# Differential-attention scores of layer 0 as three products of rounded and low parts, with the low parts kept in the residual tiles and tile 1's scores computed beside tile 3's

## The chip, the cores and the metric

One core of one Trainium2 chip runs the whole program. The metric is the device time of one execution in microseconds (us); the time before is the median of 3 runs, 1106.02 us (1105.82 to 1106.52). One further execution was taken by the profiler, and every duration below is from it.

## What is computed

The reference is a decoder trunk of two layers on 512 tokens of width 1024 in float32. Layer 0 runs latent attention (8 heads) and differential attention (4 heads) side by side behind one input projection, joins their outputs in one output projection, adds the result to the residual stream `x`, and is followed by a gated ConvFFN. Layer 1 has other attentions and the same ConvFFN. The change lies in the differential attention of layer 0:

```python
def block(args):
    i, a1, a2 = args                 # one tile of 128 queries, two query halves
    dist = (qpos[:, None] - kpos[None, :]).astype(jnp.float32)
    bias = -slopes[:, None, None] * dist
    def probs(qb, kf):
        s = jnp.einsum('bhqd,bhkd->bhqk', qb, kf).astype(jnp.float32) * scale + bias
        return jax.nn.softmax(jnp.where(causal, s, -jnp.inf), axis=-1)
    p = probs(a1, k1) - lam * probs(a2, k2)
    return jnp.einsum('bhqk,bhkd->bhqd', p.astype(v.dtype), v)
...
x = x + rms_norm(h, ev_post_g[j])    # after the output projection
```

## The kernel before

The tokens are four tiles of 128 (`i` = 0 to 3, `NT` = 4). `X[i]` is a tile's row of the residual stream (128 x 1024 float32), kept in SBUF from its first load (`load_x`, L141) until layer 0's attention output is added to it.

**Products.** TensorE multiplies plain float32 operands directly (an f32 matmul), or float32r operands, which are float32 numbers rounded to fewer bits. `mm3` (L318 to L322) makes an accurate product of rounded operands: high x high, then the two products with one high and one low part, where low = value - high. Weights come as raw tiles over SP's DMA queue (`wraw<-`, L61, three raw buffers of 512 KB), are cast to `wh` on ScalarE (L83, ACT) and give `wl` by a subtract on VectorE (L84, DVE). Activations that are used so are cut by `split` (L225 on ACT, L226 on DVE).

**The stage.** `even()` (L860) is layer 0's attention. Its differential heads run from about 112 to 200 us in 16 units `n` = (head `h`, query tile `i`), four heads with `i` in the order 3, 2, 0, 1, and four more iterations that drain. PE, DVE, ACT and POOL execute it in the order in which the loop at L1389 writes it; the DMA issues on SP stand outside that order, and a scheduler places them. One iteration `n` issues:

1. `score(n)` (L1256): for both halves `z` an f32 matmul of 64 contraction rows (row group `z`) into one PSUM bank each, `sps<-dqk` (L1265); 128 queries by (i+1)*128 keys. The unit `i` = 2 computes tile 0's scores as well, in columns 384 to 512 of its banks, and the unit `i` = 0 only picks them up. DVE adds the distance term and finds the minimum (L1275).
2. perhaps a weight cast and subtract (L83, L84).
3. `exps(n)` on ACT (L1282).
4. `fill(before)`: steps of work that does not depend on the heads at hand. A step is one `mm3` of 512 columns, or three matmuls. First come the query and key projections of heads 1 to 3 (`qk_parts`, `aqk`, eight steps each, closed by one DVE operation L1360 that writes `dqk`), then the output projection (`parts_of`, `ao`), whose weights `ev_w_out` arrive meanwhile.
5. `turn(n-1)`: transposes `tpp<-ident,s` (L891) of the combined weights; `value(n-2)`: `o<-dv,pt` (L1300), its scaling and squares on ACT, `rr` on POOL (L1307), and one long POOL DMA (L163) that prepares the ConvFFN's weights in DRAM.
6. `fill(behind)`; `norm(n-4)` on DVE (`otok`, L1314); `combine(n)` on DVE (L1287 to L1289), which gives `s` to the transposes of the next iteration; every fourth time `finish` of a head (L1321).

`plan` holds the pair (before, behind) of each iteration: (6, 2), then eleven times (2, 2), four times (2, 1), and the drain. The projections of head 0 (`diff_qk`, L1029) stand in an earlier part of `even()`, near 40 to 50 us. After the loop the output projection ends tile by tile (3, 2, 1, 0), its result is normed and added to `X[i]` (L1441), and `X[i]` is spilled to DRAM (L617).

Of the kernel before, what the change touches and what calls it, by code (L numbers as in the profile page):

```python
# [9 lines left out]
F32 = mybir.dt.float32  # L10
# [87 lines left out]
def trunk(tc, A, out):  # L98
# [3 lines left out]
    with ExitStack() as top:  # L102
# [757 lines left out]
        def even():  # L860
            with ExitStack() as es:
                ap = es.enter_context(tc.tile_pool(name="ea", bufs=1, reuse_waits="tile"))
                dqk = [ap.tile([P, 2, S], F32, tag=f"dqk{h}", name=f"dqk{h}") for h in range(4)]
                dq, dk = [t[:, 0] for t in dqk], [t[:, 1] for t in dqk]
                dv = ap.tile([P, NT, 512], F32, tag="dv", name="dv")
                oM = (ap.tile([P, 4, S], F32R, tag="omh", name="omh"),
                      ap.tile([P, 4, S], F32R, tag="oml", name="oml"))

                zero = dqk[0][:, 0, :P]
# [30 lines left out]
                with ExitStack() as e1:  # L900
# [137 lines left out]
                    with e2:  # L1038
                        qtab = cp.tile([P, 2, S], F32, tag="qtab", name="qtab")
# [216 lines left out]
                def score(h, i):  # L1256
                    if i == ORDER[0]:
                        otoks[h] = sc.tile([P, NT, P], F32, tag="otok", name="otok2", bufs=2)
                    w = (i + 1) * P
                    if i:  # L1260
                        ps = [bank("s", "sps") for _ in range(2)]
                        for j, c in ((2, slice(0, 384)), (0, slice(384, 512))) if i == 2 else ((i, slice(0, w)), ):
                            for z in range(2):
                                r = slice(z * 64, (z + 1) * 64)
                                PE.matmul(ps[z][:, c], dq[h][r, j * P:(j + 1) * P], dk[h][r, :c.stop - c.start],  # L1265
                                          start=True, stop=True)
                        if i == 2:
                            ahead[h] = [p[:, 384:] for p in ps]
                        ps = [p[:, :w] for p in ps]
                    else:  # L1270
                        ps = ahead.pop(h)
# [79 lines left out]
                def qk_parts(h, z):  # L1351
                    acc = bank("a", "aqk")
                    wh, wl = W.next()
                    for k in range(KD):
                        mm3(acc, wh[:, k * P:(k + 1) * P], wl[:, k * P:(k + 1) * P], xh[:, k], xl[:, k],
                            k == 0, k == KD - 1)
                        if k < KD - 1:
                            yield
                    scale = 1.0 if z else -0.125 / SLOPES[h]
                    DVE.scalar_tensor_tensor((dk if z else dq)[h], acc, scale, r_row, ALU.mult, ALU.mult)  # L1360
                    yield


# [17 lines left out]

                units = [(h, i) for h in range(4) for i in (3, 2, 0, 1)]
                moves = sum_steps(0, range(3, 5))
                scored, turned_, valued = {}, {}, {}
# [612 lines left out]
```

## Time and profile before

| | us |
|---|---|
| median of 3 runs | 1106.02 |
| profiled execution, its time | 1108.29 |
| its span, first to last instruction | 1106.5 |
| mean granted TensorE clock | 0.998 |
| TensorE busy | 1097.4 (99%) |
| VectorE busy | 896.6 (81%) |
| ScalarE busy | 641.4 (58%) |
| DMA, mean rate | 197 GB/s |

The profiled execution is 2.27 us above the median; 1.8 us of it lie outside the span. A row of the timeline gives the start in us, the length in us, the engine, the kernel's line, the operation, output<-inputs, the shapes and the count of instructions; in brackets the idle time before it and what ended it. Consecutive matmuls overlap in these rows, so that what one costs is read from start to start. PEld is the weight load of TensorE, which runs beside the matmul before it. SPq is SP's sequencer, with the moment at which a transfer is issued.

### The profile page before, as it was taken

The page shows a single profiled execution, that of the slowest core. Times are in us where ns is not written, and L with a number is a line of the kernel's source. Part 1 is how long each engine was busy: PE and PEld are TensorE (multiplying, and loading weights), DVE is VectorE, ACT ScalarE, POOL GpSimd, SP SyncE. Part 2 cuts the span into 40 slices and gives each one's busy share as a digit, 9 for nine tenths or more (in the row PEclk, how much of TensorE's full clock was granted, in tenths as well). Part 3 has the DMA queues.
Part 4 walks back from the last instruction along what each step waited for, and adds up shares of the span by engine and source line. Part 5 has one row for each costly group of instructions (what it writes and reads, how often), then busy time and mean ns, then how long its engine had stood idle before and what let it go on. Part 6 is the DMA issues. An engine that isn't in the chain of part 4 may idle for free.

```text
span 1106.5 us, 17950 instructions
## 1 busy us (share of the span) xinstructions
PE 1097.4 (99%) x6688; PEld 955.6 (86%) x6688; DVE 896.6 (81%) x1509; ACT 641.4 (58%) x1094; POOL 129.2 (12%) x246
## 2 busy tenths in 40 slices
PE   9999999999999999999999999999999999999997
PEld 8876777898999999888878877788999999988886
DVE  6666676489899999999874765458989999999897
ACT  6555566346666666556544555556566666656562
POOL 3311143320000000000032111014100000000002
PEclk9999999999999999999999999999999999999999
DMA  7897898458456555354627999858656555535462
GB/s 273 255 239 210 228 282 236 109 188 219 159 182 191 175 188 181 124 179 136 236 96 259 288 289 299 228 167 246 197 161 191 177 181 186 184 123 161 152 208 78
DMA packets 72600, 217.51 MB, mean 197 GB/s; under 512 B 10048, under 2 KB 11200, under 8 KB 64320
## 3 DMA queue, kind: packets, MB, share of 16 engines
q1 hardware_dynamic: 61872, 147.99, 40.3%
q0 software_dynamic: 9920, 67.12, 24.1%
q10 hardware_dynamic: 720, 1.25, 0.4%
q8 instruction: 53, 0.87, 0.3%
q14 instruction: 35, 0.29, 0.1%
HBM read 208.95 MB, written 73.43 MB: 255 GB/s over the span
## 4 chain that ended last, share of the span: by engine, by line
PE 89%; DVE 6%; DMA 2%; ACT 1%; issue 1%; POOL 0%; POOLq 0%; DVEq 0%; ACTq 0%; SPq 0%
PE u L322 12%; PE u L320 12%; PE u L321 12%; PE acc L321 4%; PE acc L320 4%; PE acc L322 4%; PE apt L320 3%; PE apt L321 3%; PE apt L322 3%; PE ao L320 2%; PE ao L322 2%; PE ao L321 2%; PE aqk L320 1%; DVE wl L84 1%; PE p L321 1%; PE p L320 1%
## 5 line engine op out<-in xcount | busy, mean ns | idle before, releaser
L84 DVE TENSOR_TENSOR wl<-wraw,wh 128x1024 fp32r<-128x1024 f32 x246 | 298.0, 1218 | 34.3 <-ACT wh L83 33.8
L83 ACT CAST wh<-wraw 128x1024 fp32r<-128x1024 f32 x246 | 254.2, 1046 | 102.4 <-PE u L321 21.5
L322 PE MATMUL u<-xh,wl 128*128 128x256 f32 (+1 forms) x640 | 194.9, 305 | 0.0
L321 PE MATMUL u<-xl,wh 128*128 128x256 f32 (+1 forms) x640 | 194.7, 304 | 0.0
L320 PE MATMUL u<-xh,wh 128*128 128x256 f32 (+1 forms) x640 | 194.5, 305 | 0.0
L322 PEld LDWEIGHTS u<-xh,wl 128*128 128x128 f32 x640 | 122.3, 191 | 5.5 <-DVE wl L84 0.7
L321 PEld LDWEIGHTS u<-xl,wh 128*128 128x128 f32 x640 | 122.3, 191 | 4.9
L320 PEld LDWEIGHTS u<-xh,wh 128*128 128x128 f32 x640 | 122.2, 191 | 5.0
L320 PE MATMUL u<-gh,wh 128*128 128x256 f32 x384 | 108.7, 283 | 0.0
L322 PE MATMUL u<-gh,wl 128*128 128x256 f32 x384 | 108.7, 283 | 0.0
L321 PE MATMUL u<-gl,wh 128*128 128x256 f32 x384 | 108.7, 283 | 0.0
L321 PE MATMUL acc<-wl,gh 128*128 128x512 f32 (+1 forms) x234 | 90.9, 389 | 0.1
L322 PE MATMUL acc<-wh,gl 128*128 128x512 f32 (+1 forms) x234 | 90.7, 387 | 0.0
L320 PE MATMUL acc<-wh,gh 128*128 128x512 f32 (+1 forms) x234 | 90.3, 388 | 0.0
L233 POOL TENSOR_TENSOR rv<-ms,epst 128x1 f32<-128x1 f32 x31 | 12.4, 399 | 617.8 <-ACT junk L287 286.2
L484 ACT ACTIVATE y<-u,cw 128x512 f32<-128x512 f32 x88 | 67.6, 776 | 27.5 <-PE u L322 27.5
L321 PEld LDWEIGHTS u<-gl,wh 128*128 128x128 f32 x384 | 73.7, 192 | 0.1
L320 PEld LDWEIGHTS u<-gh,wh 128*128 128x128 f32 x384 | 73.7, 192 | 0.1
L322 PEld LDWEIGHTS u<-gh,wl 128*128 128x128 f32 x384 | 73.7, 192 | 0.0
L163 POOL DMA_DIRECT2D ws<-in_ffn_up_q x72 | 51.7, 720 | 158.7 <-DMA ws<-ws 81.9
L490 DVE SCALAR_TENSOR_TENSOR y<-u,cw,y 128x510 f32<-128x510 f32 x88 | 65.5, 746 | 2.2
L488 DVE SCALAR_TENSOR_TENSOR y<-u,cw,y 128x511 f32<-128x511 f32 x88 | 64.9, 742 | 0.8 <-ACT y L484 0.8
(382 smaller groups left out, 2458.6 us busy)
## 6 DMA issues: line engine op xcount, KB each, us to landing
ws<-in_ffn_up_q POOLq DMA_DIRECT2D x48, 768.0 KB, 12.8
wraw<-ws SPq DMA_DIRECT2D x128, 256.0 KB, 2.9
wraw<-in_ffn_up_q SPq DMA_DIRECT2D x96, 256.0 KB, 2.9
wraw<-in_ffn_w_down SPq DMA_DIRECT2D x44, 512.0 KB, 3.6
ws<-ws POOLq DMA_DIRECT2D x16, 768.0 KB, 13.1
ws<-in_ffn_up_q POOLq DMA_DIRECT2D x24, 512.0 KB, 7.4
wraw<-in_ffn_w_up SPq DMA_DIRECT2D x24, 512.0 KB, 4.4
wraw<-in_od_w_dqk SPq DMA_DIRECT2D x12, 512.0 KB, 9.2
```

The lines of the kernel that those rows point to most:

```text
L83: self.nc.scalar.copy(h[:, :w], raw[:, :w])
L84: self.nc.vector.tensor_tensor(l[:, :w], raw[:, :w], h[:, :w].bitcast(F32), ALU.subtract)
L163: nc.gpsimd.dma_start(tiles[j][c][:].rearrange(wide, q=4), src.rearrange(wide, q=4), accum_op=op, max_dma_last_dim=8192)
L233: POOL.tensor_tensor(v[:, :n], ms, eps[:, :n], ALU.add)
L320: PE.matmul(o, lh, rh, start=first, stop=False, skip_group_check=more)
L321: PE.matmul(o, lh, rl, start=False, stop=False, skip_group_check=more)
L322: PE.matmul(o, ll, rh, start=False, stop=last, skip_group_check=more)
L484: ACT.activation(y[:, z], u[z], AF.Identity, bias=c[:, 3:4], scale=c[:, 2:3])
L488: DVE.scalar_tensor_tensor(y[:, z, 1:], u[z][:, :S - 1], c[:, 1:2], y[:, z, 1:], ALU.mult, ALU.add)
L490: DVE.scalar_tensor_tensor(y[:, z, 2:], u[z][:, :S - 2], c[:, 0:1], y[:, z, 2:], ALU.mult, ALU.add)
```

## The change

1. `dqk` (rounded parts) becomes float32r. A low part of the same shape, `dqkl`, is put for head `h` in the SBUF space of the residual tile X3, X2, X1, X0 (in this order of heads). `put_qk` replaces the one closing operation of a projection: DVE writes the value to a scratch tile, ACT casts it to `dqk`, and DVE subtracts to get `dqkl`; inside the stage the subtract stands behind `combine` of the same iteration (`to_split`).
2. Each f32 score matmul becomes three f32r products.
3. For heads 0 to 2 tile 1's scores are computed in the unit of tile 3, in two banks of the projections' and normed rows' tags ("n", "a"). Head 3 computes them in its own unit. `plan` has (3, 1) in the place of (2, 2) at n = 3, 7 and 11.
4. The residual tiles' first contents are lost, so that `back(i)` loads the four rows of `x` again, 512 KB each. It is written at n = 13, 15 and 17 and behind the loop.

```diff
@@ even()
-                dqk = [ap.tile([P, 2, S], F32, tag=f"dqk{h}", name=f"dqk{h}") for h in range(4)]
-                dq, dk = [t[:, 0] for t in dqk], [t[:, 1] for t in dqk]
+                dqk = [ap.tile([P, 2, S], F32R, tag=f"dqk{h}", name=f"dqk{h}") for h in range(4)]
+                dqk_low, to_split = [], []
...
+                    def put_qk(h, z, acc):
+                        if len(dqk_low) == h:
+                            dqk_low.append(glob.tile([P, 2, S], F32R, tag=f"X{ORDER[h]}", name="dqkl"))
+                        v = chp.tile([P, D], F32, tag="s", name="vqk")[:, :S]
+                        high, low = dqk[h][:, z], dqk_low[h][:, z]
+                        DVE.scalar_tensor_tensor(v, acc, 1.0 if z else -0.125 / SLOPES[h], r_row, ALU.mult, ALU.mult)
+                        ACT.copy(high, v)
+                        to_split.append(lambda: DVE.tensor_tensor(low, v, high.bitcast(F32), ALU.subtract))
@@ diff_qk(h, z)
-                        scale = 1.0 if z else -0.125 / SLOPES[h]
-                        DVE.scalar_tensor_tensor((dk if z else dq)[h], acc, scale, r_row, ALU.mult, ALU.mult)
+                        put_qk(h, z, acc)
+                        to_split.pop()()
@@ score(h, i)
-                    if i:
-                        ps = [bank("s", "sps") for _ in range(2)]
-                        for j, c in ((2, slice(0, 384)), (0, slice(384, 512))) if i == 2 else ((i, slice(0, w)), ):
-                            for z in range(2):
-                                r = slice(z * 64, (z + 1) * 64)
-                                PE.matmul(ps[z][:, c], dq[h][r, j * P:(j + 1) * P], dk[h][r, :c.stop - c.start],
-                                          start=True, stop=True)
...
+                    if (h, i) not in ahead:
+                        parts = {3: [(3, "ss", 0), (1, "na", 0)], 2: [(2, "ss", 0), (0, None, 384)]}.get(i, [(i, "ss", 0)])
+                        for j, tags, at in parts[:1] if i == 3 and h == 3 else parts:
+                            if tags:
+                                ps = [bank(tag, "sps") for tag in tags]
+                            ahead[h, j] = [p[:, at:at + (j + 1) * P] for p in ps]
+                            qk = dqk[h], dqk_low[h]
+                            for a, b in ((0, 0), (0, 1), (1, 0)):
+                                for z in range(2):
+                                    r = slice(z * 64, (z + 1) * 64)
+                                    PE.matmul(ahead[h, j][z], qk[a][r, 0, j * P:(j + 1) * P], qk[b][r, 1, :(j + 1) * P],
+                                              start=not a and not b, stop=a == 1)
+                    ps = ahead.pop((h, i))
@@ qk_parts(h, z)
-                    DVE.scalar_tensor_tensor((dk if z else dq)[h], acc, scale, r_row, ALU.mult, ALU.mult)
+                    put_qk(h, z, acc)
@@ the loop
-                plan = ((6, 2),) + ((2, 2),) * 11 + ((2, 1),) * 4 + ((1, 0), (1, 1), (1, 2), (0, 2))
+                plan = ((6, 2),) + ((2, 2), (2, 2), (3, 1), (2, 2)) * 2 + ((2, 2), (2, 2), (3, 1))
+                plan += ((2, 1),) * 4 + ((1, 0), (1, 1), (1, 2), (0, 2))
...
+                        while to_split:
+                            to_split.pop(0)()
+                        if n in (13, 15, 17):
+                            back(ORDER[n // 2 - 6])
...
+                back(0)
```

**SP's order, before:** the six last loads of the output weights (`wraw_` and a running number), each waiting for its buffer.

```order
L61 DMA wraw_1671<-in_ev_w_out 128x1024 [waits DMAHW2_49,DVE_49]
L61 DMA wraw_1723<-in_ev_w_out 128x1024 [waits DMAHW3_49,DVE_49]
L61 DMA wraw_1783<-in_ev_w_out 128x1024 [waits DMAHW7_49,DMAHW4_49,DVE_49]
L61 DMA wraw_1833<-in_ev_w_out 128x1024 [waits DMAHW5_49,DMAHW0_49,DVE_49]
L61 DMA wraw_1880<-in_ev_w_out 128x1024 [waits DMAHW6_49,DVE_49]
L61 DMA wraw_2105<-in_ev_w_out 128x1024 [waits DMAHW7_49,DVE_49]
```

**SP's order, after:** the same six loads, and the first two reloads that stand among or behind them (`X2_`, `X1_`).

```order
L61 DMA wraw_1725<-in_ev_w_out 128x1024 [waits DMAHW2_49,DVE_49]
L61 DMA wraw_1776<-in_ev_w_out 128x1024 [waits DMAHW7_49,DMAHW4_49,DVE_49]
L141 DMA X2_2235<-in_x 128x1024 [waits DMAHW0_49,PE_49]
L61 DMA wraw_1848<-in_ev_w_out 128x1024 [waits DMAHW5_49,DVE_49]
L61 DMA wraw_1910<-in_ev_w_out 128x1024 [waits DMAHW6_49,DVE_49]
L61 DMA wraw_1957<-in_ev_w_out 128x1024 [waits DMAHW7_49,DMAHW3_49,DVE_49]
L61 DMA wraw_2199<-in_ev_w_out 128x1024 [waits DMAHW1_49,DVE_49]
L141 DMA X1_2281<-in_x 128x1024 [waits PE_49]
```

X2's reload, written at n = 15, stands ahead of three output-weight loads, two places behind the load that is first here; it waits for PE only (the last score that reads head 1's low part). X1's stands behind all of them. X3's reload stands three loads ahead of X2's, and X0's ahead of the last of the first three `ffn_w_up` loads.

**DVE's order, before**, around the end of the key projection of head 3 (unit n = 10): `dqk_95` is head 3's tile, `s` the combined weights, 128x256 the distance terms of the unit behind it.

```order
L84 TENSOR_TENSOR wl<-wraw,wh 128x1024
L1360 SCALAR_TENSOR_TENSOR dqk_95<-aqk,dist 128x512
L1314 SCALAR_TENSOR_TENSOR otok_1564<-otok_1564,rr,subg 128x128
L1287 RECIPROCAL st<-st 128x2
L1288 SCALAR_TENSOR_TENSOR st<-st,neglam 128x1
L1289 SCALAR_TENSOR_TENSOR s<-s,st 128x128
L1275 ISA s,st<-sps,dist 128x256
```

**DVE's order, after**, at the same place.

```order
L84 TENSOR_TENSOR wl<-wraw,wh 128x1024
L1034 SCALAR_TENSOR_TENSOR vqk<-aqk,dist 128x512
L1324 SCALAR_TENSOR_TENSOR otok_1594<-otok_1594,rr,subg 128x128
L1297 RECIPROCAL st<-st 128x2
L1298 SCALAR_TENSOR_TENSOR st<-st,neglam 128x1
L1299 SCALAR_TENSOR_TENSOR s<-s,st 128x128
L1036 TENSOR_TENSOR dqkl<-vqk,dqk_95 128x512
L1285 ISA s,st<-sps,dist 128x256
```

The subtract `dqkl` stands between `combine` and the distance terms of the next unit; what is ahead of `combine` is the same.

**PE's order, after**, at the start of head 2 (`dqk_94`), where before one row, `L1265 MATMUL sps<-dqk_94 128x512 x2`, stood.

```order
L1279 MATMUL sps<-dqk_94 128x512 x2
L1279 MATMUL sps<-dqkl,dqk_94 128x512 x2
L1279 MATMUL sps<-dqk_94,dqkl 128x512 x2
L1279 MATMUL sps<-dqk_94 128x256 x2
L1279 MATMUL sps<-dqkl,dqk_94 128x256 x2
L1279 MATMUL sps<-dqk_94,dqkl 128x256 x2
L320 MATMUL aqk<-xh,wh 128x512
```

Twelve matmuls stand in the place of two, the first six for tile 3 and the others for tile 1, whose own block three units later is gone.

More of the change, by code (lines that the diff above doesn't have):

```diff
@@ L867, in even @@
                       ap.tile([P, 4, S], F32R, tag="oml", name="oml"))
-                zero = dqk[0][:, 0, :P]
+                zero = dqk[0][:, 0, :P].bitcast(F32)
                 DVE.memset(zero, 0.0)
@@ L1259, in score @@
                     w = (i + 1) * P
-                    if i:
-                        ps = [bank("s", "sps") for _ in range(2)]
-                        for j, c in ((2, slice(0, 384)), (0, slice(384, 512))) if i == 2 else ((i, slice(0, w)), ):
-                            for z in range(2):
-                                r = slice(z * 64, (z + 1) * 64)
-                                PE.matmul(ps[z][:, c], dq[h][r, j * P:(j + 1) * P], dk[h][r, :c.stop - c.start],
-                                          start=True, stop=True)
[L1267 to L1271, printed above, removed]
+                    if (h, i) not in ahead:
[11 more added lines that the diff above has]
+                    ps = ahead.pop((h, i))
                     st = sc.tile([P, 8], F32, tag="st", name="st", bufs=11)
@@ L1358, in qk_parts @@
                             yield
-                    scale = 1.0 if z else -0.125 / SLOPES[h]
-                    DVE.scalar_tensor_tensor((dk if z else dq)[h], acc, scale, r_row, ALU.mult, ALU.mult)
+                    put_qk(h, z, acc)
                     yield
@@ L1383, in even, with back @@
                 moves = sum_steps(0, range(3, 5))
+                def back(i):
+                    X[i] = glob.tile([P, D], F32, tag=f"X{i}", name=f"X{i}")
+                    load_x(i)
                 scored, turned_, valued = {}, {}, {}
-                plan = ((6, 2),) + ((2, 2),) * 11 + ((2, 1),) * 4 + ((1, 0), (1, 1), (1, 2), (0, 2))
+                plan = ((6, 2),) + ((2, 2), (2, 2), (3, 1), (2, 2)) * 2 + ((2, 2), (2, 2), (3, 1))
+                plan += ((2, 1),) * 4 + ((1, 0), (1, 1), (1, 2), (0, 2))
                 depth, W.depth = W.depth, 0
```

## Prediction

> **What bounds the kernel now.** The busy times come first, then the stage's stretches, then the timeline of PE at the score blocks.
>
> ```profile
> PE 1097.4 (99%) x6688; PEld 955.6 (86%) x6688; DVE 896.6 (81%) x1509; ACT 641.4 (58%) x1094; POOL 129.2 (12%) x246
> ```
>
> PE is busy for 99% of the span: what PE is spared or made to wait is the first account. The stage with the differential heads, in three stretches (start:end, length, busy time and count of PE, PEld, DVE, ACT and POOL, granted clock, DMA share, GB/s):
>
> ```profile
> 112.00:140.00 28.00, 28.00 (x141) 19.19 (x139) 17.73 (x52) 16.84 (x42) 2.23 (x4) 1.00 0.89 235
> 140.00:165.00 25.00, 25.00 (x138) 18.97 (x138) 20.15 (x54) 17.33 (x49) 11.22 (x23) 1.00 0.95 283
> 165.00:190.00 25.00, 25.00 (x140) 19.05 (x139) 16.64 (x57) 16.83 (x55) 8.75 (x18) 1.00 0.89 229
> ```
>
> PE never rests here, at a granted clock of 1.00. But the DMA engines are busy for 0.89, 0.95 and 0.89 of it: a second bound, close under the first, and the change adds 2 MB of loads to it. VectorE and ScalarE have air, about 0.2 to 0.4 of each stretch.
>
> **The score blocks on PE.** What a block costs is the step from the start of the matmul before it to the start of the second one behind it, less two ordinary steps.
>
> ```profile
> 138.32 0.39 PE L321 MATMUL aqk<-xl,wh 128*128 128x512 f32 x1
> 138.55 0.40 PE L322 MATMUL aqk<-xh,wl 128*128 128x512 f32 x1
> 138.88 1.13 PE L1265 MATMUL sps<-dqk 64*128 64x512 f32 x4
> 139.94 0.50 PE L320 MATMUL aqk<-xh,wh 128*128 128x512 f32 x1
> 140.27 0.40 PE L321 MATMUL aqk<-xl,wh 128*128 128x512 f32 x1
> ...
> 134.50 0.70 PE L1265 MATMUL sps<-dqk 64*128 64x256 f32 x4
> 135.13 0.50 PE L320 MATMUL aqk<-xh,wh 128*128 128x512 f32 x1
> ...
> 143.34 1.14 PE L1265 MATMUL sps<-dqk 64*128 64x384 f32 x8
> 144.41 0.50 PE L320 MATMUL aqk<-xh,wh 128*128 128x512 f32 x1
> ...
> 113.52 1.12 PE L1265 MATMUL sps<-dqk 64*128 64x512 f32 x2
> 114.57 1.09 PE L1151 MATMUL tpp<-ident,s 128*128 128x128 f32 x8
> ```
>
> An ordinary step of 512 f32r columns is 0.23 (138.55 - 138.32); the steps into a block and behind it are 0.33, 0.10 longer each. So tile 3's block costs 140.27 - 138.55 - 0.46 = 1.26, of which 1.06 lie between its start and the next one. Tile 1's lies 0.63 inside, with the same 0.20 around it 0.83; tile 2's (with tile 0's) 1.07 inside, 1.27 in all. The last pair of rows is one half `z` alone (x2, not x4): it takes 1.05, as much as both halves in 138.88. So the two row groups run side by side. A block also has a fixed part: 256 more columns cost 1.06 - 0.63 = 0.43, so that 512 cost 0.86 and 0.20 inside are fixed (0.21 in tile 2's); with the 0.20 around I take 0.42 per block, since a block after has more matmuls.
>
> The steps of narrower f32r matmuls:
>
> ```profile
> 629.16 0.27 PE L1601 MATMUL cp<-sl,tri 128*128 128x128 f32 x1
> 629.27 0.33 PE L1601 MATMUL cp<-sh,tri 128*128 128x256 f32 x1
> 629.44 0.28 PE L1601 MATMUL cp<-sl,tri 128*128 128x256 f32 x1
> 629.55 0.22 PE L1594 MATMUL run<-sh,tri 128*128 128x128 f32 x1
> ```
>
> 128 columns step by 0.11, 256 by 0.17 and 0.11. I take 0.11 for 256 and 0.17 for 384. If the pairs of f32r products share the array as the f32 ones do, a block costs three steps and the fixed 0.42:
> - heads 1 and 2, tiles 3 and 1 together: 3 x 0.23 + 3 x 0.11 + 0.42 = 1.44 against 1.26 + 0.83 = 2.09: -0.65 each, -1.3.
> - head 0: its first block is in two pieces, one half `z` ahead of other work (113.52) and one behind it, some 1.25 each, with tile 1's 0.83 together 3.33; after, the first products of both halves stand ahead (0.23 + 0.42 = 0.65) and the rest behind (2 x 0.23 + 3 x 0.11 + 0.42 = 1.21), 1.86: -1.47.
> - head 3: 3 x 0.23 + 0.42 = 1.11 against 1.26, and 0.76 against 0.83: -0.22.
> - tile 2 with 0: 3 x (0.17 + 0.11) + 0.42 = 1.26 against 1.27: nothing, four times.
>
> PE's sum is **-3.0 us**. Nothing in these rows excludes that f32r pairs run one after the other; then each head has 3 x (0.23 + 0.11 + 0.17 + 0.11) = 1.86 more, 7.45 in all, and the sum is +4.5.
>
> The row behind this is that tile 2's block, with twice the matmuls (x8) and thus twice the weight loads of tile 3's (x4), takes 1.07 inside against 1.06: no load is seen. The Trainium skill, "TensorE: Matmul & The Clock Gate", section "Part 3: Packing small matmuls — row/col tiling", says that a weight load overlaps a running matmul only where the row group differs. By that rule the six loads of a block alternate between two groups that are both at work, and an estimate of one bare load of 0.11 for each of 48 pairs would be 5.3, so that PE's sum would be +2.3 and not -3.0.
>
> **The split of the projections.** Eight casts on ACT and eight subtracts on DVE are added; ACT is idle for a third of each stretch.
>
> ```profile
> 120.03 0.69 DVE L226 TENSOR_TENSOR oml<-o,omh 128x512 fp32r<-128x512 f32 x1 [2.98 <-ACT omh L225]
> ...
> 130.38 0.62 DVE L1289 SCALAR_TENSOR_TENSOR s<-s,st 128x384 f32<-128x384 f32 x1
> 131.56 0.48 PEld L891 LDWEIGHTS tpp<-ident,s 128*128 128x128 f32 x3
> ```
>
> A subtract of 128x512 takes 0.69, about 0.61 to the next start. Those of the stage stand behind `combine`, and so push the distance terms of the next unit, which is tile 2's in each head. That unit's `combine` ends at 131.00 and its transposes load at 131.56: 0.56 of air against 0.61, thus 0 to 0.3 for each of three heads, in all 0.2 (added to nothing else below, since it lies where PE has gained already). Head 0's splits stand where DVE waits for PE anyway:
>
> ```profile
> 48.66 0.69 DVE L1101 TENSOR_TENSOR mq<-auq,qtab 128x512 f32<-128x512 f32 x1 [2.03 <-PE auq L322]
> ```
>
> 2.03 idle covers 0.61; if it didn't, two times 0.6 would come on top.
>
> **The reload of X2.** Here stands the term that decides. The three loads of output weights behind it, and their casts:
>
> ```profile
> 147.63 0.33 SPq L61 DMA_DIRECT2D wraw<-in_ev_w_out  x1
> 150.73 0.33 SPq L61 DMA_DIRECT2D wraw<-in_ev_w_out  x1
> 155.88 0.33 SPq L61 DMA_DIRECT2D wraw<-in_ev_w_out  x1
> ```
>
> ```profile
> wraw<-in_ev_w_out SPq DMA_DIRECT2D x1, 512.0 KB, 8.9
> ...
> wraw<-in_ev_w_out SPq DMA_DIRECT2D x1, 512.0 KB, 10.2
> ...
> wraw<-in_ev_w_out SPq DMA_DIRECT2D x1, 512.0 KB, 10.9
> ```
>
> ```profile
> 157.66 1.05 ACT L83 CAST wh<-wraw 128x1024 fp32r<-128x1024 f32 x1
> 161.51 1.03 ACT L83 CAST wo<-wraw 128x1024 fp32r<-128x1024 f32 x1
> 166.84 1.05 ACT L83 CAST wh<-wraw 128x1024 fp32r<-128x1024 f32 x1
> ```
>
> Issue plus time to landing: 156.53, 160.93 and 166.78. The casts start at 157.66, 161.51 and 166.84: air of 1.13, 0.58 and 0.06. The landings are 4.40 and 5.85 apart, each for 512 KB at a DMA share of 0.95. X2's reload is as large, stands ahead of these three on SP, and is free to go when PE has read head 1's low part for the last time (tile 2's block, done at 144.41), before 147.63. It pushes the three by x. At least 0, where it fills gaps; at most a whole turn, 5.85. In 25 us a share of 0.95 leaves 1.25 of gaps, so that most of a turn is someone's: I take **x = 4.4**, the shorter spacing.
>
> The Trainium skill, "DMA: Bandwidth & Descriptors", section "Queues, rings and completion order", says that an engine takes turns between the queues it has work for, packet by packet; X2 then costs its queue a full turn, as a mean of the two spacings 5.1, and the sum below would end 0.7 later. The spacings agree with it as far as they go.
>
> What the last load holds up, on DVE and PE:
>
> ```profile
> 167.93 1.23 DVE L84 TENSOR_TENSOR wl<-wraw,wh 128x1024 fp32r<-128x1024 f32 x1 [0.45 <-ACT wh L83]
> 170.58 0.69 DVE L1360 SCALAR_TENSOR_TENSOR dqk<-aqk,dist 128x512 f32<-128x512 f32 x1 [1.42 <-PE aqk L322]
> ...
> 171.89 0.35 DVE L1289 SCALAR_TENSOR_TENSOR s<-s,st 128x128 f32<-128x128 f32 x1
> ...
> 172.60 0.27 PE L891 MATMUL tpp<-ident,s 128*128 128x128 f32 x1
> ```
>
> Landing 166.78 + x, the cast 1.04, the subtract 1.23 less some 0.09 (170.58 - 1.42 = 169.16 is its end, and operations that follow without a wait start a little before the end of the last), then 1.66 from L1360 to the end of L1289 (172.24 - 170.58): `combine` is done at 170.6 + x. PE takes the transposes at 172.60, some 0.1 behind their release at the earliest, so that PE is late by x - 1.9 against this trace, whatever it has gained before. With x = 4.4 that is +2.5. From it go 0.69 (`plan` now has three steps ahead of the transposes at n = 11 and one behind them, so a step that PE did later is done while it waits), and 0.22 of head 3, which comes later still: +1.6.
>
> The DMA side itself may come earlier. PE reaches these units up to 1.47 + 0.65 sooner, and buffers come free sooner; but that lead is held by POOL:
>
> ```profile
> 141.34 0.79 POOL L163 DMA_DIRECT2D ws<-in_ffn_up_q  x1 [5.86 <-DMA ws<-ws]
> 142.61 0.56 POOL L1307 TENSOR_TENSOR rr<-st,mhalf 128x1 f32<-128x1 f32 x1
> 144.06 0.34 DVE L1314 SCALAR_TENSOR_TENSOR otok<-otok,rr,subg 128x128 f32<-128x128 f32 x1
> ```
>
> POOL waits 5.86 for an earlier transfer and only then makes `rr`, ready at 143.17, which DVE needs at 144.06 ahead of `combine`: 0.89 of lead at most can pass. X3's reload, in the same DMA engines, may hold POOL longer. I count half, 0.5, off the sum: **+1.1**.
>
> X3's, X1's and X0's own waits cost nothing on PE by themselves: X3's and X1's tiles are free before SP comes to them, and X0's last reader is head 3's last scores. X0 is first needed by the last tile's norm, with what is behind it bounded by 0 to 1.2: it shares the DMA engines with the ends of the heads, where a late `otok` already holds PE:
>
> ```profile
> 198.35 0.31 PEld L1321 LDWEIGHTS tpo<-ident,otok 128*128 128x128 f32 x3 [0.35 <-DVE otok L1314]
> ```
>
> I take 0 for it, since 0.35 is all that shows there, and keep 1.2 for the range.
>
> Sum: +1.1 against the profiled execution, 1108.29 to 1109.4 (its span 1106.5 to 1107.6). The median of the runs lies 2.27 lower: **1107.1 us**.
>
> **The rivals.**
> 1. The reload is hidden (x under 0.7): X2's packets displace POOL's transfers and not the weights. For it: POOL's queue moves more bytes here than SP's, and its transfers have no reader in this stage. Against it: air of 0.06 at the last cast. Then PE's -3.0 stands, less 0.4 for the subtracts and POOL's hold: -2.6, **1103.4**. The two cases meet at x - 3.3 = -2.6.
> 2. Slower, by a whole turn and more: X2 goes ahead of its three loads in full and meets POOL's, x from 5.5 up: 5.85 - 3.3 is +2.55, and with X0's tail up to 1.2 more: +2.2 to +3.7, about **1108.9**. For it: share 0.95, landings 10.9 behind their issue. Against it: 1.25 of gaps.
> 3. Slower, by bare weight loads, PE's sum +2.3, which hides most of the wait for X2: **1108.3**. Against it stands the row of tile 2 (x8 at 1.07).
> 4. Slower, by f32r halves one after the other: PE's sum +4.5, **1110.5**; it decides from a pair's step above 0.23 + 0.04. Against it: 113.52 beside 138.88, in f32.
>
> That the change doesn't do what it says can be left out: PE's rows in the built order show the twelve matmuls, and SP's the reloads.
>
> **How the numbers follow.** The forecast (x of 1.6 to 5.4, 1104 to 1108.2) has 0.44, the first rival 0.25, the second 0.13, the third 0.08, the fourth 0.10. A measurement of this kernel can tell about 0.2%, 2.2 us, from no change. Faster by over that, below 1103.8: the first rival and the lower edge of the forecast, 0.27. Slower, above 1108.2: the second, half of the third, the fourth, and the forecast's upper edge: 0.28. Between: 0.45. For 8 in 10 the range leaves out the fourth rival and the ends of the first: 1103.2 to 1109.8.
>
> **What the profile after would show.** The score block of tiles 3 and 1 near 1.2 us inside, and tile 2's near 1.07, if the halves run side by side; near 2 and 1.9 if not; over 1.6 with bare loads. The three output-weight loads land later by 4 to 5 than before, ACT's casts wait for `wraw`, DVE's `combine` of n = 10 is late, and PE shows about 2 us of waiting for `s` around 172 to 176. If PE never waits there, the first rival is right. POOL's `rr` of the fifth unit shows whether the lead is held. The prediction is wrong as a whole if PE waits at another place: for a low part that is cast too late, or for a residual row at the end.

## The result, and the profile after

| | us | against before |
|---|---|---|
| before, median of 6 runs | 1106.04 (1105.78 to 1106.52) | |
| after, median of 6 runs | 1110.62 (1108.56 to 1112.81) | 1.0039 (95%: 1.0029 to 1.0049) |
| after, second series, 11 runs | 1108.43 (1105.99 to 1109.99) | 1.0016 (1.0007 to 1.0025) |
| profiled execution after | 1111.42, span 1109.3 | before: 1108.29, span 1106.5 |

The change costs time: 4.6 us in the first series, 1.9 in the second; the forecast was 1.1. Before, the runs lie within 0.74 us of each other in this table, after within 4 and more; beside the second series, 33 runs of before lie within 3.4. The rows of after for the last two of the prediction's stretches, and for the one behind them (same columns); the row of before for that last one stands first:

```profile
190.00:210.00 20.00, 20.00 (x96) 16.05 (x95) 6.35 (x12) 7.40 (x22) 6.20 (x14) 1.00 0.68 182
```

```profile
140.00:165.00 25.00, 24.40 (x148) 19.43 (x147) 20.65 (x54) 17.22 (x49) 11.91 (x23) 1.00 1.01 306
165.00:190.00 25.00, 23.95 (x143) 19.05 (x142) 17.45 (x57) 18.33 (x59) 8.50 (x18) 1.00 0.90 246
190.00:210.00 20.00, 18.38 (x80) 14.06 (x79) 6.09 (x12) 5.05 (x16) 5.73 (x13) 0.91 0.66 182
```

PE, which never rested here before, now rests for 0.6, 1.05 and 1.62 us, and in the last stretch its granted clock falls to 0.91. The DMA share went from 0.95 to 1.01 in the first of them and hardly moved in the others (0.89 to 0.90, 0.68 to 0.66). First the block that the prediction priced (tiles 3 and 1 of head 1, timeline of PE):

```profile
137.37 0.40 PE L322 MATMUL aqk<-xh,wl 128*128 128x512 f32 x1
137.69 0.50 PE L1279 MATMUL sps<-dqk 64*128 64x512 f32 x2
138.03 0.40 PE L1279 MATMUL sps<-dqkl,dqk 64*128 64x512 f32 x2
...
138.94 0.50 PE L320 MATMUL aqk<-xh,wh 128*128 128x512 f32 x1
139.28 0.40 PE L321 MATMUL aqk<-xl,wh 128*128 128x512 f32 x1
```

It costs 139.28 - 137.37 - 0.46 = 1.45 (inside 1.25), forecast 1.44. In the same way tile 2's block is 1.20 (1.26 before), head 3's 0.1 less each; over the stage the blocks take **3.05 us** less, as forecast. But PE then waits in four places:

```profile
155.42 1.01 PE L1331 MATMUL tpo<-ident,otok 128*128 128x128 f32 x4 [0.46 <-ACT pt L894]
168.35 0.52 PE L891 MATMUL tpp<-ident,s 128*128 128x128 f32 x3 [1.05 <-DVE s L1299]
199.94 0.55 PE L1331 MATMUL tpo<-ident,otok 128*128 128x128 f32 x3 [1.41 <-DVE otok L1324]
201.17 0.50 PE L320 MATMUL ao<-wh,odh 128*128 128x512 f32 x1 [0.21 <-ACT odh L225]
```

Ahead of the second one, X2's reload and the casts that wait for the loads behind it (SP, then ACT):

```profile
143.50 0.33 SPq L141 DMA_DIRECT2D X<-in_x  x1
```

```profile
158.55 1.05 ACT L83 CAST wh<-wraw 128x1024 fp32r<-128x1024 f32 x1 [1.49 <-DMA wraw<-in_ev_w_out]
164.65 1.05 ACT L83 CAST wo<-wraw 128x1024 fp32r<-128x1024 f32 x1 [2.16 <-DMA wraw<-in_ev_w_out]
167.99 1.03 ACT L83 CAST wh<-wraw 128x1024 fp32r<-128x1024 f32 x1
```

The wait at 168.35 stands behind the second of these loads: it is in front of the three transposes of tile 2 (n = 9), one unit ahead of the place that the prediction priced. There (n = 10, one transpose, behind the third load) PE waits for nothing in this trace:

```profile
173.04 0.28 PE L891 MATMUL tpp<-ident,s 128*128 128x128 f32 x1
```

Ahead of the third wait, POOL stands in its queue in front of a transfer that waits for another, with the last `rr` behind it (before, the same transfer waits 1.45 and starts at 196.18):

```profile
197.77 0.87 POOL L163 DMA_DIRECT2D ws<-in_ffn_up_q  x1 [2.91 <-DMA ws<-ws]
198.94 0.56 POOL L1317 TENSOR_TENSOR rr<-st,mhalf 128x1 f32<-128x1 f32 x1
```

And behind it the clock (rows of PE, then two short stretches):

```profile
202.48 0.63 PE L320 MATMUL ao<-wh,odh 128*128 128x512 f32 x1
202.91 0.63 PE L321 MATMUL ao<-wl,odh 128*128 128x512 f32 x1
```

```profile
198.00:201.50 3.50, 1.88 (x9) 1.02 (x8) 0.70 (x2) 0.59 (x1) 2.24 (x4) 1.00 0.64 101
201.50:205.00 3.50, 3.50 (x9) 2.48 (x8) 1.03 (x2) 0.69 (x2) 0.18 (x1) 0.53 1.03 213
```

A step of 512 columns is 0.43 for some 3 us in place of 0.23, at a granted clock of 0.53; PE counts as busy meanwhile. Step for step the after trace is 0.18 later than before's at the first score block, 0.17 at the last head's `tpo` (198.26 against 198.09), some 1.8 behind the two waits and 3.1 behind the slow stretch (where the ConvFFN's first products start).

So one number serves for all that follows: **the stage**, from the start of the first score block to the start of the last head's transposes. Before it is 113.52 to 198.09. It is read from one profiled execution; the ratio is from all runs. The *lead* of a trace at some row is how much earlier than in before's trace that row starts.

| kernel | stage, us | ratio to before (95%) |
|---|---|---|
| before; before_2 | 84.57; 84.55 | |
| after; after_2 | 84.56; 84.22 | 1.0039; 1.0016 |
| no_reload | 83.47 | 1.0005 (0.9996 to 1.0013) |
| no_x0 | 84.18 | 1.0019 (1.0010 to 1.0027) |
| x2_late | 83.51 | 1.0013 (1.0003 to 1.0023) |
| tail_move | 86.84 | 1.0013 (1.0002 to 1.0023) |
| x2_late_tail | 83.49 | 1.0001 (0.9992 to 1.0010) |
| sp_hand; sp_hand_2 | 83.54; 88.08 | 1.0070 (1.0050 to 1.0091); one execution |
| sub_late; best | 82.94; 82.84 | 1.0007 (0.9998 to 1.0017); 1.0006 (0.9997 to 1.0014) |
| fin_late; best_fin | 82.72; 82.86 | 0.9990 (0.9981 to 0.9999); 1.0005 (0.9996 to 1.0013) |
| merge_only; merge_fin | 83.86; 83.66 | 0.9991 (0.9982 to 1.0000); 0.9993 (0.9984 to 1.0002) |

### The profile page after: what moved, and what is told of

It reads as the page before. It is cut to its first block, busy times and chain, and to the rows that moved or that the text cites. A ratio compares the mean times of both kernels' runs of the same rounds, so it can differ in the third digit from the quotient of the medians.

```text
span 1109.3 us, 18036 instructions
## 1 busy us (share of the span) xinstructions
PE 1097.1 (99%) x6720; PEld 958.4 (86%) x6720; DVE 901.3 (81%) x1517; ACT 646.2 (58%) x1102; POOL 129.3 (12%) x246
## 3 DMA queue, kind: packets, MB, share of 16 engines
q10 hardware_dynamic: 720, 1.25, 0.4%
## 4 chain that ended last, share of the span: by engine, by line
PE 90%; DVE 3%; issue 2%; DMA 2%; ACT 1%; POOL 1%; POOLq 0%; DVEq 0%; ACTq 0%; SPq 0%
PE u L322 12%; PE u L321 12%; PE u L320 12%; PE acc L320 5%; PE acc L321 5%; PE acc L322 5%; PE apt L320 3%; PE apt L321 3%; PE apt L322 3%; PE ao L322 1%; PE ao L320 1%; PE ao L321 1%; PE p L321 1%; PE p L320 1%; PE p L322 1%
```

## The experiments

**The reloads taken away, all or one.** In both kernels the residual add takes the normed output in place of a row of `x` that isn't reloaded.

```diff
 def back(i):
     X[i] = glob.tile([P, D], F32, tag=f"X{i}", name=f"X{i}")
-    load_x(i)
+    if i in RELOAD:          # no_reload: (), no_x0: (3, 2, 1)
+        load_x(i)
```

> The changed kernel without the four reloads of the residual rows; the residual add of layer 0's attention takes the normed output twice in place of the row of x, on the same engine with the same shapes. Theory A (the loss is DMA: the reloads push the output weights and POOL's transfers): the time falls under that of before, to 1103 to 1105 us, and PE waits neither for s near 168 us nor for otok near 199 us. Rival B (the loss is the split, eight casts and eight subtracts more on ACT and DVE, and the score blocks): it stays at 1108 us or more.

Measured: 1106.73 beside 1106.31 before, ratio 1.0005. The waits near 168 and 199 us are gone, as theory A said; but the time is not under that of before, which it also asked (1103 to 1105). It lies between the bounds of the two theories: the reloads are most of the loss in time, and 1.95 of PE's 3.05 us are lost without them (stage 83.47, not 81.5).

> The changed kernel without the last of the four reloads only (tile 0's residual add takes the normed output in place of the row of x). Theory A1 (X0's reload, issued near 187 us, delays the transfer for which POOL waits ahead of the last rr): about 3 us less than the changed kernel, 1107 to 1108, and PE's wait for otok near 199 us goes back to some 0.35 us. Rival A2 (all reloads together push POOL's chain of transfers): under 1 us less. Rival A3 (X2's displacement is the loss, as the prediction had it): no change.

Measured: 1108.70, ratio 1.0019, PE's wait for `otok` 0.72, and one of 0.48 for `s` at 172.32, the place that the prediction priced. X0's reload by itself is not the loss.

**The change once more**, beside the next three.

> The changed kernel once more, on the same chip as the three beside it, with a second profile. Every theory expects the time that it had, 1109 to 1112. Theory A (the reloads' transfers collide with the output weights and with POOL's transfers, by an amount that changes from run to run): the second profile shows other lengths for the same two waits, at the transposes for s near 168 us and at otok near 199 us. Rival B (the split and the score blocks): the waits are the same in both to 0.1 us.

Measured: 1108.43, under what every theory expected. The second profile has 0.62 for `s` (after: 1.05) and no wait at the last `tpo` (after: 1.41), but the same 0.46 near 155 us. So the two collisions differ from run to run, and the first wait doesn't.

**X2's reload behind the output weights.** SP joins the hand-written order; X3's place and that of two other loads is kept by hand.

```diff
-with tc.manual_schedule(engines={PE.engine, DVE.engine, ACT.engine, POOL.engine}):
+with tc.manual_schedule(engines={PE.engine, DVE.engine, ACT.engine, POOL.engine, nc.sync.engine}):
...
-                        if n in (13, 15, 17):
-                            back(ORDER[n // 2 - 6])
+                        if n in (3, 15, 17):
+                            back({3: 3, 15: 2, 17: 1}[n])
```

> The changed kernel with X2's reload behind all output-weight loads, beside X1's, and nothing else moved on any engine. Theory A3 (X2's displacement is a large part of the loss): no wait for s near 168 us, and 1.5 to 3 us less than the changed kernel. Theory A1 (the tail holds what is ahead of it): the waits near 168 us go, but the end of the stage waits for POOL's transfers all the longer, and the time stays within 1 us of the changed kernel or rises.

Measured: 1107.39, 1.0 under after_2, less than A3 asked; no wait for `s` is left, and the stage is 0.7 shorter than after_2's. The casts of the three weights, to be read against after's 158.55, 164.65 and 167.99:

```profile
156.89 1.05 ACT L83 CAST wh<-wraw 128x1024 fp32r<-128x1024 f32 x1
162.30 1.05 ACT L83 CAST wo<-wraw 128x1024 fp32r<-128x1024 f32 x1
166.61 1.03 ACT L83 CAST wh<-wraw 128x1024 fp32r<-128x1024 f32 x1
```

Against this execution, after's casts are 1.7, 2.4 and 1.4 later. Not all of that need be X2: in no_reload, which has no reload, they come at 156.41, 162.11 and 167.10 with the stage 0.47 earlier, so 0.0, 0.3 and 1.0 later than here. The wait at the last `tpo` is there (0.87), as A1 had it.

**POOL's transfer behind the last `rr`**, alone and with the above.

```diff
-                            if moves:
-                                moves.pop(0)()
+                            if moves and n != 16:
+                                for _ in range(1 + (n == 17)):
+                                    moves.pop(0)()
```

> The changed kernel with one POOL transfer (the one written at n = 16) issued behind the last rr instead of ahead of it; all loads as they were. If PE's wait for otok near 199 us, with the low granted clock behind it, comes from POOL standing in its queue in front of that transfer, the time falls by about 3 us to 1107 to 1108. If the wait has another source, or the low clock comes by itself, it falls by under 1.5.

> The kernel before this one, and in addition POOL's transfer of n = 16 behind the last rr. If the two places (X2 ahead of the output weights, and POOL's wait for a transfer at the end) hold the whole loss, the time falls to 1105 or less, under that of before, and PE waits neither near 168 us nor near 199 us. If the split on ACT and DVE holds much of it, it stays at 1106.5 or more.

Measured: tail_move 1108.62 (ratio 1.0013), 2.0 under the first series of after and 0.2 above the second, so that the time alone decides nothing. There is no wait at the last `tpo`; but its profile, of the slowest of 12 runs, shows the loads behind X2 at their latest, the third too (ACT, then PE):

```profile
158.04 1.05 ACT L83 CAST wh<-wraw 128x1024 fp32r<-128x1024 f32 x1 [0.99 <-DMA wraw<-in_ev_w_out]
165.06 1.05 ACT L83 CAST wo<-wraw 128x1024 fp32r<-128x1024 f32 x1 [2.62 <-DMA wraw<-in_ev_w_out]
171.25 1.05 ACT L83 CAST wh<-wraw 128x1024 fp32r<-128x1024 f32 x1 [2.75 <-DMA wraw<-in_ev_w_out]
```

```profile
168.77 0.52 PE L891 MATMUL tpp<-ident,s 128*128 128x128 f32 x3 [1.47 <-DVE s L1299]
175.28 0.30 PE L891 MATMUL tpp<-ident,s 128*128 128x128 f32 x1 [1.65 <-DVE s L1299]
```

The third cast is 4.6 later than in x2_late, and PE waits behind the second load and behind the third. x2_late_tail: 1106.69, 1.7 under after_2, ratio 1.0001; the stage is that of no_reload (83.49), with all four reloads. Both collisions are gone, and it isn't under before: what is left lies elsewhere, as the expectation's second case had it. Of the six profiles with reloads and this transfer in its old place, five wait at the last `tpo` (0.44 to 1.41); of the four where it stands behind `rr`, none.

**SP in the order of the loop.** As x2_late, but with `back` left at 13, 15 and 17.

> The changed kernel with SP's order as written in the loop: X3's reload behind three more output-weight loads, X2's and X1's behind all of them; nothing else moves. Theory A3 (X2's displacement of the output weights): the casts wait no longer for raw weights, PE's wait for s near 168 us goes, and the time falls by 1 to 2.5 us, to 1108 to 1109.6. Theory A1 or A2 (the tail): no gain or a loss, 1110 to 1112, since the reloads now lie nearer to the transfers that POOL waits for near 195 us.

> The kernel sp_hand once more, for a profile of an execution that is nearer to its median of 1115 us; the first profile showed 1107.8. If the loss is in the stage with the heads, the waits for s or for otok are longer there than in any profile so far, by 5 us or more in all; if it lies elsewhere, the stage is as in the first profile.

"Nothing else moves" was wrong: the loads of `g_post` and `gain` moved too, from ahead of the output weights to among them. Measured: 1114.98, above what either theory expected; the second profile, of an execution at 1113.72, shows where (ACT, then PE):

```profile
162.18 1.05 ACT L83 CAST wh<-wraw 128x1024 fp32r<-128x1024 f32 x1 [5.08 <-DMA wraw<-in_ev_w_out]
```

```profile
166.61 0.73 PE L891 MATMUL tpp<-ident,s 128*128 128x128 f32 x4 [2.86 <-DVE s L1299]
...
168.43 0.63 PE L321 MATMUL aqk<-xl,wh 128*128 128x512 f32 x1
168.85 0.63 PE L322 MATMUL aqk<-xh,wl 128*128 128x512 f32 x1
```

A weight is 5 us late, PE idle for 2.86, and the low clock is there again behind it. The first profile, of the same program with the same order of issues at 1107.8, has none of this; so the order with two more loads ahead of the weights is not enough by itself, and what decides between the two stays open.

**A second profile of before.**

> The kernel before, for a second profile: the first one ran 2.27 us above the median of its runs. Theory A (the time of the stage with the differential heads is the same in every execution of the kernel before, and what differs lies elsewhere): the step from the first score block near 113.5 us to the transposes of the last head near 198 us is 84.6 us again, within 0.2. Rival: the stage itself is shorter by 1 to 2 us in an execution at the median, so that the lead of the changed kernels in it was an artefact of the first profile.

Measured: 84.55, and no wait of PE between 110 and 240 us. Theory A holds in these two profiles: the stage is the same, and what varies lies elsewhere, above all at layer 0's end, near 561 us, where PE waits 1.04 in the first profile and 0.36 in the second. The other kernels differ there as well: no_reload waits 0.99, fin_late not at all.

**Where PE's lead goes.** First the merge by itself, in f32.

```diff
                             for z in range(2):
                                 r = slice(z * 64, (z + 1) * 64)
-                                PE.matmul(ps[z][:, c], dq[h][r, j * P:(j + 1) * P], dk[h][r, :c.stop - c.start],
+                                PE.matmul(ahead[h, j][z], dq[h][r, j * P:(j + 1) * P], dk[h][r, :(j + 1) * P],
                                           start=True, stop=True)
```

> The kernel before with one part of the change: tile 1's scores beside tile 3's (heads 0 to 2) and the changed plan, in plain f32, without low parts and without reloads. From the rows of before a block's fixed 0.4 us is saved three times: PE has 1.2 us less to do. Theory A1 (the end of the stage waits for POOL's chain of transfers, which PE's lead doesn't move): 0 to 0.5 us less than before. Rival (PE bounds the stage to its end): 1.2 us less, 1105.1.

Measured: 1105.99, 0.5 under before, ratio 0.9991; stage 0.7 shorter, not 1.2. At the end of head 0 its lead falls from 0.91 (155.63 for 156.54) to 0.06 at the next transposes: 0.43 of that are tile 1's scores, now made in this block, and the other 0.42 is lost, with 0.12 more at the end of head 1. So part of the loss needs neither low parts nor reloads.

Then the subtract, moved on DVE from behind `combine` to behind the next unit's `otok` (on no_reload, and on x2_late_tail as "best").

```diff
+                        due = len(to_split)
                         if n < len(units):
                             a = score(*units[n])
...
+                        for _ in range(due):
+                            to_split.pop(0)()
                         if n < len(units):
                             scored[n] = combine(a)
-                        while to_split:
-                            to_split.pop(0)()
```

> The kernel no_reload (the changed kernel without the four reloads; the residual add of layer 0's attention takes the normed output twice), with the subtract that makes the low part moved on DVE by most of a unit: behind otok of the next unit instead of ahead of that unit's distance terms. Theory C (at the ends of heads 0 and 1 PE's lead is held by the chain from the end of a projection over DVE and ACT to the transposes tpo, which the subtract lengthens by 0.6 us): the wait in front of tpo near 155 us falls from 0.45 by most of it, the stage from the first score block to the last tpo gets shorter by 0.4 to 1.2 us, and the time by as much, to 1105.5 to 1106.3. Rival D (the cover is gone with tile 1's block, and DVE's weight subtract ahead of otok decides): 0 to 0.3 us.

> All four reloads as in x2_late_tail (X2 behind the output weights, POOL's transfer of n = 16 behind the last rr), with the subtract moved as in sub_late. If theory C holds and the reloads' collisions are over, it beats x2_late_tail by 0.4 to 1.2 us and before by 0.3 to 1: 1105.3 to 1106.2. If D holds, it stays at x2_late_tail's 1106.7.

Measured: the wait in front of `tpo` is gone in both. From the transposes behind head 1's first block to those behind head 2's, sub_late loses 0.58 less than no_reload, and from there to head 3's 0.58 less again; but a new wait, ahead of both, costs 0.55:

```profile
138.94 0.50 PE L1280 MATMUL sps<-dqkl,dqk 64*128 64x512 f32 x2 [0.30 <-DVE dqkl L1037]
```

The stage is 0.53 shorter (82.94), as theory C had it, and the time is not: 1106.77 and 1106.72. In both profiles the stage starts late (114.13 and 114.23, against 113.16 in no_reload), with waits of PE for its first weights near 9.5 us (0.49 and 0.73) ahead of it; whether other executions do so too is not known.

Last the ends of heads 0 to 2, written behind the next score block (on no_reload; on x2_late_tail as "best_fin"; on merge_only with POOL's transfer moved too as "merge_fin").

```diff
                         if n < len(units):
                             a = score(*units[n])
+                        if n in (8, 12, 16):
+                            finish(n // 4 - 2)(None)
...
-                        if n >= 7 and n % 4 == 3:
-                            finish(n // 4 - 1)(None)
+                        if n == 19:
+                            finish(3)(None)
```

> The kernel no_reload (no reloads; the residual add takes the normed output twice) with the end of heads 0 to 2, the transposes tpo and the cut of their result, moved from the end of a head's last unit to behind the next score block. Theory C+D (the 1.95 us of PE's 3.05 that no_reload loses are lost in front of tpo, half by the subtract on the chain, half by the cover that went with tile 1's block): no wait in front of tpo near 155 us, and the stage from the first score block to the last tpo falls from 83.47 to 81.4 to 82.2 us. Rival E (the loss is spread over PE's small waits for weights and banks): 83.1 or more.

> The change with all its arithmetic and reloads, and three moves: X2's reload behind the output weights, POOL's transfer of n = 16 behind the last rr (both as in x2_late_tail), and the ends of heads 0 to 2 behind the next score block as in fin_late. Theory: the stage at 81.4 to 82.2 us, the time 1.3 to 2 us under x2_late_tail, 1104.7 to 1105.5, under that of before. Rival: PE's lead is taken again by a later wait (the chain at the end of the stage, or a transfer elsewhere), and the time stays at 1106 or more.

> The kernel merge_only (plain f32, no low parts, no reloads, tile 1's scores beside tile 3's) with the same two moves: ends of heads behind the next score block, POOL's transfer behind the last rr. It has 1.2 us less on PE than before and nothing more on DMA, ACT or DVE. Theory: the stage at 83.2 to 83.5 us (merge_only 83.86), the time 1105.0 to 1105.6. Rival: no change against merge_only's 1106.0.

Measured: no wait in front of `tpo`, and in its place one at the next transposes:

```profile
158.56 0.44 PE L892 MATMUL tpp<-ident,s 128*128 128x128 f32 x2 [0.35 <-DVE odl L227]
```

fin_late's stage is 82.72, 0.75 shorter than no_reload's: less than C and D asked, more than E allowed. Of PE's 3.05 us, 1.2 are still missing: some 0.5 and 0.3 of them at the same two ends of heads. fin_late is the one kernel with f32r scores under before (1105.56 beside 1106.46), without reloads. best_fin has nearly the same stage with them (82.86) and takes 1107.05; merge_fin has 83.66, more than expected, and takes 1106.06. best_fin's trace is 2.2 ahead of before's at 240 us and 1.2 at the end: 0.6 of it goes at layer 0's end, where PE waits 0.28 near 546 us and 0.99 near 561 (before's first profile 1.04, its second 0.36, both near 561). The rival holds there, and merge_fin's rival too. No version was found that beats before by more than 0.1%.

## Why the prediction was wrong

- **The blocks: right.** -3.05 for -3.0; halves side by side (1.25 inside, not 2), so the serial rival is out. The Trainium skill's rule on weight loads ("TensorE: Matmul & The Clock Gate", Part 3) would have put the block at over 1.6 inside; the measurement decides against bare loads here, at least for pairs of two row groups in turn (steps of 0.23 and 0.12 a pair).
- **The split, "in all 0.2": the step that failed first.** It took the unit behind each subtract for tile 2's "in each head". Six subtracts stand in the stage, two for each of three heads: after has them at 127.54, 144.46 and 163.09 ahead of the distance terms of tile 2 (128x384), and at 135.66, 153.06 and 172.78 ahead of those of tile 1 (128x256), as DVE's order ahead of the prediction shows for one of these. The second three were left out, and two of them lengthen a chain that ends at the end of a head: from the end of a projection over `combine`, the next unit's distance terms and exponentials on ACT to the copy `pt`, which frees the PSUM bank of `tpo`. Before, then after:

```profile
152.36 0.69 DVE L1360 SCALAR_TENSOR_TENSOR dqk<-aqk,dist 128x512 f32<-128x512 f32 x1 [1.66 <-PE aqk L322]
...
155.41 0.24 ACT L894 COPY pt<-tpp 128x128 f32<-128x128 f32 x1
156.54 0.60 PE L1321 MATMUL tpo<-ident,otok 128*128 128x128 f32 x4
```

```profile
151.47 0.69 DVE L1034 SCALAR_TENSOR_TENSOR vqk<-aqk,dist 128x512 f32<-128x512 f32 x1 [1.14 <-PE aqk L322]
...
153.06 0.68 DVE L1036 TENSOR_TENSOR dqkl<-vqk,dqk 128x512 fp32r<-128x512 f32 x1
...
155.12 0.24 ACT L894 COPY pt<-tpp 128x128 f32<-128x128 f32 x1
```

  The chain is 3.05 before (155.41 - 152.36) and 3.65 after. Beside it PE had 4.18 (`tpo` at 156.54) and has 0.84 less since tile 1's block is gone: 3.34. Air of 1.13 became a lack of 0.31, and `otok` comes later still. By no_reload the two ends of heads (0 and 1) cost 1.20 and 0.75, together **1.95 for 0.2**; sub_late shows 1.16 of it to be the subtract, merge_only that the lost cover takes 0.5 without it. The rest, some 0.3, was not taken apart. PE's waits at `tpo` are at "another place", as the prediction's last sign has it, but for neither of the two causes that it names there. Head 0's splits, priced at nothing, add 0.3 ahead of the stage: from the first `auq` product near 43 us to the first score matmul near 59 all 13 profiles with f32r scores take 16.6 (16.58 to 16.64) and all four without take 16.32. The 2.03 of idle time stands ahead of a later `mq`; the subtract of the key projection (45.07) stands between two operations that followed without a wait, and `mq` behind it starts at 45.67 (45.22 before).
- **X2's reload: the mechanism right, its size and its place not.** Forecast x = 4.4 at the third cast; against x2_late it is 1.4 in after and 4.6 in tail_move. The prediction listed the air of all three loads and followed only the last, whose air of 0.06 was the least. In after and after_2 PE waits behind the second load (air 0.58) and not behind the third; no_x0 waits behind the third alone, tail_move behind both. (By the prediction's own sign, no wait around 172 to 176, after's trace would speak for the first rival; it waited one unit earlier.) PE's loss was 1.2 in after (its lead of 0.61 became a lag of 0.59), 0.8 in after_2 and 3.3 in tail_move. So the reload was priced too high for two of these three, and it comes on top of the 1.95, which the sum had put at 0.2. The full turn, 5.1, that the prediction derives from the Trainium skill ("DMA: Bandwidth & Descriptors", section "Queues, rings and completion order") lies above all six delays that after and tail_move show against x2_late (1.2 to 4.6).
- **The end of the stage, "0 for it, since 0.35 is all that shows": the second step that failed.** A reload was weighed by its own reader, with 1.2 kept for the range; what the reloads delay is POOL's chain of transfers, and POOL's queue holds the last `rr`. In after 1.6 of waits and 1.3 of low clock, 2.9 for 0. It isn't X0's place alone (no_x0 0.72, x2_late 0.87, no_reload 0).
- **POOL's hold on the lead:** `rr` is ready at 142.07 in after (141.51 + 0.56), 1.1 earlier than before, and PE's lead there is 0.97. The bound of 0.89 gave way, to no effect.

For after's profile: -3.05 + 1.95 + 1.2 + 2.9, with 0.2 from ahead of the stage, is 3.2; the traces stand 3.1 apart at 230 us. Forecast and first series differ by 3.5 us; 2.2 of it lie between two series of the same kernel, whose profiles differ in the two collisions and in little else. That the second series ends near the forecast (1.9 slower for 1.1) is luck: its profile (of an execution at 1107.5) has -3.05, 1.95 and 0.8 in the stage, 0.3 ahead of it and no collision at the end, while the forecast had most of its loss in X2's reload. What is not settled is why no_reload's shorter stage (by 1.1) ends at no gain in its runs: 0.3 goes to head 0's splits, and the rest is no more than the waits outside the stage vary by (at layer 0's end alone from 0 to 1.04 in these profiles). Its own trace does keep a lead of 1.4 over before's to the end; but that profile of before ran 2.27 above its median, and before_2's trace, of the same kernel, ends 1.1 ahead of it too.

## What to carry to other kernels

Work that PE is spared is a gain only where no chain ran beside it with less air; list the chains that end at the next waits, with their air, before counting the block. An operation added on an engine that is idle for a third of the time is not free when it stands in such a chain. Where DMA engines were busy for 0.95 of a stretch, a load with no urgent reader still had a victim, by an amount that changed from run to run; placed behind the urgent loads, and with POOL's transfer moved, the same four loads cost the stage nothing (x2_late_tail beside no_reload). An engine that waits in its queue for a transfer holds whatever stands behind it, here `rr` behind 2.91 us.

## What the runs showed of the hardware

In two of the 17 profiles PE's granted clock fell to about half for some 3 us while PE had work, each time behind PE's longest rest in the stage: after (1.41 idle, 1.68 from the start of the matmul before, then 0.53 of the clock from 201.5 to 205) and sp_hand_2 (2.86 idle, steps of 0.43 from 168 to 170). tail_move's rests of 1.47 and 1.65 had no such sequel, so that no threshold can be read from these. The Trainium skill ("TensorE: Matmul & The Clock Gate", Part 1) puts the fall to half rate behind an idle window of about 3.4 us; here it came behind 2.86 once, and behind less than half of the page's figure the other time. The wait at the end of after's stage thus cost 2.9 where its idle time shows 1.6.
